# An encoder layer on one core: the weights of the last product prepared at another place, and in part not prepared

## The chip, the core and the metric

The kernel runs on one core of a Trainium2 chip. The metric is the device time of one execution in microseconds (us). The kernel before took 1651.42 us (median of 3 runs, 1650.65 to 1651.42). The engines of the core are named as in the profile: PE multiplies matrices (PEld is its loading of weights), DVE, ACT and POOL compute element by element, SP only issues transfers (DMA).

## The reference

Two sequences of 512 tokens with 1024 channels go through one layer, each with a memory of 256 tokens:

```python
xn = rmsnorm(x); h = xn @ w_in                     # u, q, k, v, xq and three gates g
branches = (s5(u), diff_attention(q, k, v), cross_attention(xq, mem))
merged = sum(sigmoid(g[n]) * (branches[n] @ w_up[n]) for n in range(3))
x = x + merged @ w_out
gate, up = split(rmsnorm(x) @ w_ffn_in)            # 2 x 2816 columns
y = rmsnorm(x + (silu(gate) * up) @ w_ffn_out)
```

All numbers are 32-bit floats. "The last product" below is `(silu(gate) * up) @ w_ffn_out`, 2816 x 1024 weights on 1024 tokens.

## The kernel before

Everything is held with channels along the 128 partitions and tokens along the free dimension; a matrix is a row of tiles of 128 x 1024 (512 columns for each sequence). A product of two 32-bit matrices is made of three matmuls: each operand is split into a high part, rounded by ACT (`split`, L128, or L131 where it is scaled), and a low part, what is left, subtracted by DVE (L129, or L132 where it is scaled); the matmuls high x high, high x low and low x high are summed in PSUM (L61).

The stages follow each other in the order of the code: projections, the S5 branch, cross attention, differential attention, the gated merges (`merge_units`: 24 tiles, the last eight ending in `mg`, L726, and its split `mgh`, `mgl`), the product with `w_out`, the FFN (22 steps of `for i in range(KFF)`), the last product, and a tail with four leftover tiles and the last norm.

The FFN and the last product use a form of the product of 2 x 2 blocks that takes seven block products in place of eight. One step of the FFN makes four blocks of 128 x 512 (gate and up, both sequences) out of seven sums of products; the step's activations go to DRAM (`aD[i]`, "aD<-ac"). For the last product two such tiles, 2p and 2p+1, form a pair of operands (p = 0 to 8): `act_pair` loads them back ("fa" and "fb"), `quad_sums` forms four sums of their quarters ("ts": L907, L909, L910 on DVE, L908 on POOL), and `quad_split` splits the seven blocks into "th" and "tl".

The weights of the last product come in 36 pieces (m, p): the 2 x 2 blocks A11, A12 (output tile m) and A21, A22 (output tile m+4), 128 x 128 each, against pair p. A piece gives 21 matmuls (seven products of three). `VISITS` puts the pieces into 12 visits of 2, 3 or 4 pieces; a visit keeps its seven sums in seven PSUM banks, and at its end ACT copies one of them ("p", L1041), DVE adds the others (`summed`, L1035: "u", "gf", "p", "up", "nsq"), and POOL adds the four results to the output tiles ("y", L1143). While a visit's matmuls run, DVE drains the visit before it; and since only pairs 0 and 1 are ready when the last product begins, the early visits have a pair of operands made beside them too (`pair_in`), one after visit 1, two after visit 3, one each after visits 4, 6 and 7.

A piece needs seven weight blocks: A11, A12, A22 and the four sums S1 to S4. The kernel before prepares all seven of every piece long before, in `prepare`: a piece is loaded ("raw", 4 x 128 columns), its A11, A12, A22 are split (L131, L132, "hl", 128 x 384) and stored to DRAM ("wD<-hl", 384 KB), POOL forms the four sums in place (L424 to L427, 128 x 128 each), and these are split (128 x 512) and stored (512 KB). `half_piece` takes half of that, one split with its store, wherever it is called: 16 pieces beside cross attention, 11 beside the gated merges, 9 beside the FFN's steps 1 to 18 (`NPREP`). In the last product a piece is then only two loads ("w<-wD", 384 and 512 KB) straight into the weight buffers.

The order of instructions on an engine is the order of the code, except where the scheduler of the framework moves work forward: it fills an engine's queue by what it expects to be ready, under the constraint of the buffers, while PE keeps its written order in the attentions and the merges that go with them, and from the last FFN step through the last product (`PE.on`). Buffers come from pools, and a pool on the right side takes room that another pool gave back: the "ts" buffers of the last two-and-a-half FFN steps are opened only after the pool "pq" of `prepare` is closed, at step 19. SP issues every transfer in its own queue.

## Time and profile before

One execution was profiled. Its own time was 1648.71 us, 2.71 us less than the median of the runs; its span, from the first to the last record, 1646.9 us, leaves 1.8 us around it.

| | us of the span | share |
|---|---|---|
| PE busy | 1597.5 | 97% |
| PE not busy | 49.4 | 3% |
| DVE busy | 1175.2 | 71% |
| ACT busy | 633.5 | 38% |
| POOL busy | 550.4 | 33% |
| mean granted clock of PE | 0.988 | |

PE is the engine to look at first. Where it is busy for the whole of a stage, nothing on the other engines costs anything; where it is not, or where its granted clock falls below 1, time is lost. The stages, by their place in the span: cross attention 412 to 522 us, differential attention 522 to 740 (its end to 787), the last merges 787 to 876, `w_out` to 996, the FFN to 1417, the last product to 1588, the tail to 1647.

### The profile page before, as it was taken

The page shows a single profiled execution, that of the slowest core. Times are in us where ns is not written, and L with a number is a line of the kernel's source. Part 1 is how long each engine was busy: PE and PEld are TensorE (multiplying, and loading weights), DVE is VectorE, ACT ScalarE, POOL GpSimd, SP SyncE. Part 2 cuts the span into 40 slices and gives each one's busy share as a digit, 9 for nine tenths or more (in the row PEclk, how much of TensorE's full clock was granted, in tenths as well). Part 3 has the DMA queues.
Part 4 walks back from the last instruction along what each step waited for, and adds up shares of the span by engine and source line. Part 5 has one row for each costly group of instructions (what it writes and reads, how often), then busy time and mean ns, then how long its engine had stood idle before and what let it go on. Part 6 is the DMA issues. An engine that isn't in the chain of part 4 may idle for free.

```text
span 1646.9 us, 21707 instructions
## 1 busy us (share of the span) xinstructions
PE 1597.5 (97%) x7812; PEld 1317.8 (80%) x7812; DVE 1175.2 (71%) x1860; ACT 633.5 (38%) x1130; POOL 550.4 (33%) x444
## 2 busy tenths in 40 slices
PE   7999999899999999999989999999999999999997
PEld 5788788788897778777767886888888887888887
DVE  7957897154775676766576657898998888886545
ACT  6534323245554355564233433333233332331122
POOL 0001100000333221200555344666666665344242
PEclk9999999999999999999999998999999999999998
DMA  9354343737664110145785542433333322887632
GB/s 366 123 165 150 110 157 111 233 120 249 234 231 150 52 59 22 54 144 178 241 301 166 163 130 64 145 131 105 129 118 106 119 99 94 291 322 243 213 116 102
DMA packets 109355, 259.61 MB, mean 158 GB/s; under 512 B 14016, under 2 KB 42432, under 8 KB 109248
## 3 DMA queue, kind: packets, MB, share of 16 engines
q1 hardware_dynamic: 109248, 258.23, 46.1%
q8 instruction: 61, 1.00, 0.3%
q14 instruction: 46, 0.38, 0.1%
HBM read 174.85 MB, written 83.33 MB: 157 GB/s over the span
## 4 chain that ended last, share of the span: by engine, by line
PE 79%; DVE 10%; DMA 3%; issue 2%; POOL 2%; ACT 2%; SPq 1%; DVEq 0%; POOLq 0%; ACTq 0%
PE bkmm L61 68%; PE bktr L61 3%; PE bksc L61 2%; PE bkoo L61 2%; PE bktr L64 2%; DVE wl L129 2%; DVE st L1492 1%; PE bktr L1474 1%; POOL mg L726 1%; POOL up L1089 1%; DMA yt<-bD 1%; DVE hl L132 1%; DVE xt L243 0%; DMA wD<-hl 0%; DMA raw<-in_w_fo 0%
## 5 line engine op out<-in xcount | busy, mean ns | idle before, releaser
L61 PE MATMUL bkmm<-xh,wh 128*128 128x512 f32 x640 | 255.4, 399 | 1.2 <-ACT wh L128 1.2
L61 PE MATMUL bkmm<-xh,wl 128*128 128x512 f32 x640 | 250.9, 393 | 2.3 <-DVE wl L129 2.3
L61 PE MATMUL bkmm<-xl,wh 128*128 128x512 f32 x640 | 250.6, 392 | 0.0
L61 PE MATMUL bkmm<-tl,wh 128*128 128x512 f32 (+1 forms) x621 | 243.3, 392 | 3.3 <-DVE tl L129 3.3
L61 PE MATMUL bkmm<-th,wl 128*128 128x512 f32 (+1 forms) x621 | 241.5, 390 | 3.4 <-DVE wl L129 3.4
L61 PE MATMUL bkmm<-th,wh 128*128 128x512 f32 (+1 forms) x621 | 243.2, 392 | 0.0
L129 DVE TENSOR_TENSOR wl<-wf,wh 128x1024 fp32r<-128x1024 f32 (+1 forms) x133 | 152.0, 1143 | 71.8 <-ACT wh L128 63.4
L128 ACT CAST wh<-wf 128x1024 fp32r<-128x1024 f32 (+1 forms) x133 | 117.7, 885 | 204.2 <-PE bkmm L61 138.0
L424 POOL TENSOR_TENSOR raw<-raw 128x128 f32<-128x128 f32 x36 | 22.3, 620 | 400.3 <-DVE hl L132 396.9
L61 PEld LDWEIGHTS bkmm<-xh,wh 128*128 128x128 f32 x640 | 120.3, 188 | 32.0 <-issue 7.9
L61 PEld LDWEIGHTS bkmm<-xh,wl 128*128 128x128 f32 x640 | 120.2, 188 | 29.6 <-DVE wl L129 3.1
L61 PEld LDWEIGHTS bkmm<-tl,wh 128*128 128x128 f32 x621 | 117.7, 190 | 28.4 <-DVE tl L129 4.4
L61 PEld LDWEIGHTS bkmm<-th,wl 128*128 128x128 f32 x621 | 117.2, 189 | 27.7 <-DVE wl L129 3.9
L61 PE MATMUL bkmm<-th,w 128*128 128x512 f32 x432 | 139.2, 390 | 0.0
L61 PEld LDWEIGHTS bkmm<-xl,wh 128*128 128x128 f32 x640 | 120.4, 188 | 22.4 <-issue 0.4
L61 PEld LDWEIGHTS bkmm<-th,wh 128*128 128x128 f32 x621 | 117.6, 189 | 25.6 <-ACT wh L128 1.2
L1089 POOL TENSOR_TENSOR up<-up,acc 128x512 f32<-128x512 f32 x44 | 84.6, 1942 | 93.6 <-DVE up L1035 93.6
L61 PEld LDWEIGHTS bkmm<-th,w 128*128 128x128 f32 x432 | 81.1, 188 | 17.5 <-DVE up L1035 0.7
L132 DVE SCALAR_TENSOR_TENSOR hl<-raw,hl 128x384 fp32r<-128x384 f32 (+1 forms) x72 | 72.9, 1016 | 24.0 <-ACT hl L131 23.9
L487 ACT ACTIVATE e<-bksc,nb 128x512 f32<-128x512 f32 (+1 forms) x96 | 58.8, 615 | 70.0 <-DVE nb L482 51.7
L61 PE MATMUL bkmm<-tl,w 128*128 128x512 f32 x216 | 84.1, 389 | 0.0
L61 PE MATMUL bkmm<-yh,wh 128*128 128x512 f32 x192 | 78.0, 407 | 3.3 <-DVE gl L722 2.9
(628 smaller groups left out, 3524.7 us busy)
## 6 DMA issues: line engine op xcount, KB each, us to landing
wf<-in_w_in SPq DMA_DIRECT2D x40, 512.0 KB, 3.9
wD<-hl SPq DMA_DIRECT2D x36, 512.0 KB, 2.9
w<-wD SPq DMA_DIRECT2D x36, 512.0 KB, 4.5
wD<-hl SPq DMA_DIRECT2D x36, 384.0 KB, 2.9
w<-wD SPq DMA_DIRECT2D x36, 384.0 KB, 3.4
gD<-gt SPq DMA_DIRECT2D x24, 512.0 KB, 2.9
gl<-gD SPq DMA_DIRECT2D x24, 512.0 KB, 4.0
wf<-in_w_fg SPq DMA_DIRECT2D x22, 512.0 KB, 3.5
```

The source lines that it names most:

```text
L61: return self.put(self.eng.matmul(*args, **kw))
L64: return self.put(self.eng.transpose(*args, **kw))
L128: h = S.copy(hi, src)
L129: l_ = V.tensor_tensor(out=lo, in0=src, in1=hi.bitcast(F32), op=ALU.subtract)
L132: l_ = V.scalar_tensor_tensor(out=lo, in0=src, scalar=scale, in1=hi.bitcast(F32), op0=ALU.mult, op1=ALU.subtract)
L424: PO.tensor_tensor(out=a22, in0=a21, in1=a22, op=ALU.add)
L487: last_x = S.activation(out=e, in_=sc, func=AF.Exp, bias=nb, scale=scale, accum_out=sm)
L726: PO.tensor_tensor(out=mg[m], in0=mg[m], in1=gt, op=ALU.add)
L1089: PO.tensor_tensor(out=up, in0=up, in1=accs[s], op=ALU.mult)
L1474: PE.matmul(ps[:, g * P : (g + 1) * P], w_[:, gg * P : (gg + 1) * P], u_[:, 8 * o + gg, :], start=True, stop=True)
L1492: V.tensor_tensor(out=sv[:, :, :, i], in0=p_, in1=q_, op=ALU.add)
```

## The change

`PREPARED` says how many blocks of a piece are prepared in each visit: seven for the two pieces of visit 0, four (the sums S1 to S4 alone) for the 32 pieces of visits 1 to 10, none for the two pieces of visit 11. All of this is done beside cross attention, in 36 half pieces (one more call at its beginning); `raw` gets four buffers and is loaded three pieces ahead. Beside the merges and the FFN nothing is prepared any more, and the pool "pq" is closed before differential attention.

In the last product `weights7` takes the place of `prepared`. For a piece with four blocks it loads the raw A11, A12, A22 into one of the two buffers of "acc" (128 KB + 64 KB), loads the sums from `wD` (512 KB), and one piece later, ahead of its matmuls, splits the raw blocks on ACT (L131) and DVE (L132) into the weight buffers. For the last two pieces POOL forms the sums there as well. Loads are issued two pieces ahead. Pair 4 is made after the first piece of visit 3, not after its end.

The diff, with the unchanged ends of functions left out:

```diff
@@ -36,7 +36,7 @@
           (2, 6, 9), (3, 7, 9))
 NPAIR = 9
 
-NPREP = (16, 27)
+PREPARED = (7, 4, 4, 4, 4, 4, 4, 4, 4, 4, 4, 0)
 
 NG = (7, 5, 7)
 ROUND = 12582912.0
@@ -393,39 +393,56 @@
 
 
 
-    pieces = [(m, p) for m, lo_, hi_ in VISITS for p in range(lo_, hi_)]
-    wD = {mp: drp.tile([P, 7, 2, P], F32, name=f"wD{mp[0]}_{mp[1]}") for mp in pieces}
-
-    def prepare(es_, pieces_):
+    pieces = [(m, p, PREPARED[v]) for v, (m, lo_, hi_) in enumerate(VISITS) for p in range(lo_, hi_)]
+    wD = {(m, p): drp.tile([P, n, 2, P], F32, name=f"wD{m}_{p}") for m, p, n in pieces if n}
+
+    def raw_in(raw, m, p, whole=True):
+
+        f = slice(2 * p * P, (2 * p + 2) * P)
+        nc.sync.dma_start(raw[:, 1:3], a["w_fo"][m, :, f].rearrange("p (a n) -> p a n", n=P))
+        if whole:
+            return nc.sync.dma_start(raw[:, 0::3], a["w_fo"][m + 4, :, f].rearrange("p (a n) -> p a n", n=P))
+        f = slice((2 * p + 1) * P, (2 * p + 2) * P)
+        return nc.sync.dma_start(raw[:, 3], a["w_fo"][m + 4, :, f])
+
+    def raw_sums(raw):
+
+        a21, a11, a12, a22 = (raw[:, i] for i in range(4))
+        PO.tensor_tensor(out=a22, in0=a21, in1=a22, op=ALU.add)
+        PO.tensor_tensor(out=a21, in0=a11, in1=a21, op=ALU.subtract)
+        PO.tensor_tensor(out=a11, in0=a22, in1=a11, op=ALU.subtract)
+        PO.tensor_tensor(out=a12, in0=a12, in1=a11, op=ALU.subtract)
+
+    def prepare(es_):
         pq = es_.enter_context(tc.tile_pool(name="pq", bufs=1, side="right", reuse_waits="tile"))
-        raws = []
-
-        def load(m, p):
-            raw = pq.tile([P, 4, P], F32, tag="raw", name="raw", bufs=2)
-            f = slice(2 * p * P, (2 * p + 2) * P)
-            with queued():
-                nc.sync.dma_start(raw[:, 1:3], a["w_fo"][m, :, f].rearrange("p (a n) -> p a n", n=P))
-                nc.sync.dma_start(raw[:, 0::3], a["w_fo"][m + 4, :, f].rearrange("p (a n) -> p a n", n=P))
-            raws.append(raw)
-
-        load(*pieces_[0])
+        todo_, raws = [x_ for x_ in pieces if x_[2]], []
+
+        def load():
+            if len(raws) < len(todo_):
+                raws.append(pq.tile([P, 4, P], F32, tag="raw", name="raw", bufs=4))
+                with queued():
+                    raw_in(raws[-1], *todo_[len(raws) - 1][:2])
+
+        def part(n_, j, w_):
+            m, p, _ = todo_[n_]
+            k = w_.shape[1]
+            hl = pq.tile([P, k, 2, P], F32R, tag=f"hl{k}", name="hl", bufs=k // 2)
+            split(hl[:, :, 0], hl[:, :, 1], w_, scale=0.5)
+            nc.sync.dma_start(wD[m, p][:, j : j + k], hl.bitcast(F32))
+
+        for _ in range(3):
+            load()
         yield
-        for n_, (m, p) in enumerate(pieces_):
-            raw = raws[n_]
-            if n_ + 1 < len(pieces_):
-                load(*pieces_[n_ + 1])
-            for j, w_ in ((4, raw[:, 1:4]), (0, raw)):
-                n = w_.shape[1]
-                hl = pq.tile([P, n, 2, P], F32R, tag=f"hl{n}", name="hl")
-                split(hl[:, :, 0], hl[:, :, 1], w_, scale=0.5)
-                nc.sync.dma_start(wD[m, p][:, j : j + n], hl.bitcast(F32))
-                if j:
-                    a21, a11, a12, a22 = (raw[:, i] for i in range(4))
-                    PO.tensor_tensor(out=a22, in0=a21, in1=a22, op=ALU.add)
-                    PO.tensor_tensor(out=a21, in0=a11, in1=a21, op=ALU.subtract)
-                    PO.tensor_tensor(out=a11, in0=a22, in1=a11, op=ALU.subtract)
-                    PO.tensor_tensor(out=a12, in0=a12, in1=a11, op=ALU.subtract)
+        for n_, (m, p, k) in enumerate(todo_):
+            load()
+            if k == 7:
+                part(n_, 4, raws[n_][:, 1:4])
+                raw_sums(raws[n_])
                 yield
+            part(n_, 0, raws[n_])
+            if n_ + 1 < len(todo_) and todo_[n_ + 1][2] == 4:
+                raw_sums(raws[n_ + 1])
+            yield
 
     def half_piece(behind_=()):
         with ExitStack() as es_:
@@ -534,7 +551,7 @@
     xcol = phase.enter_context(tc.tile_pool(name="xcol", bufs=2, reuse_waits="tile"))
 
     pes = ExitStack()
-    prep = prepare(pes, pieces[: NPREP[0]])
+    prep = prepare(pes)
     next(prep)
 
 
@@ -659,6 +676,8 @@
             S.copy(osb, oo)
             nc.sync.dma_start(bD[2, h, :, s * L : (s + 1) * L], osb)
         half_piece(last_e)
+        if i == -AHEAD:
+            half_piece(last_e)
     while queue:
         fill(6)
     assert next(prep, None) is None
@@ -850,11 +869,8 @@
         if i > 2 and steps[i - 3][2] == 3:
             normed(i - 3)
     aes.close()
-    prep = prepare(pes, pieces[NPREP[0] : NPREP[1]])
-    next(prep)
     while queue:
         fill(24)
-        half_piece()
     assert next(todo, None) is None
     PE.on = False
     phase.close()
@@ -869,11 +885,6 @@
     for m in range(KD):
         for _ in merge_units(1, b1, m, last=True):
             pass
-        half_piece()
-        if m < 6:
-            half_piece()
-    assert next(prep, None) is None
-    pes.close()
 
 
 
@@ -1062,12 +1073,7 @@
             w = next(wg)
             next(wg)
             next(wg)
-        if i == 1:
-            prep = prepare(pes, pieces[NPREP[1] :])
-            next(prep)
-        elif i == KFF - 3:
-            assert next(prep, None) is None
-            pes.close()
+        if i == KFF - 3:
             open_tags(ses, side="right", ts=1)
             open_tags(fes, ts2=1)
         if i == KFF - 1:
@@ -1090,8 +1096,6 @@
             V.scalar_tensor_tensor(out=ac[:, cs], in0=ac[:, cs], scalar=1.0, in1=gf, op0=ALU.add, op1=ALU.mult)
             V.tensor_tensor(out=ac[:, cs], in0=ac[:, cs], in1=up, op=ALU.mult)
         nc.sync.dma_start(aD[i], ac)
-        if 1 <= i < KFF - 3:
-            half_piece((last_t, last_sum))
 
 
 
@@ -1108,25 +1112,54 @@
 
     n_w = 0
 
-    def prepared(m, p):
-
-        nonlocal n_w, last_w
+    def w_room(n):
+        nonlocal n_w
+        n_w += 1
+        tag = ("wf", "wf", "wh", "wl", "wh", "wl")[n_w % 6]
+        return wp.tile([P, DM], F32R, tag=tag, name="w7")[:, : n * 2 * P].rearrange("p (j h c) -> p j h c", h=2, c=P)
+
+    def weights7(m, p, n):
+
+        nonlocal last_w
+        wa, ws_ = w_room(3), w_room(4)
+        raw = None
+        if n < 7:
+            raw = new_acc().rearrange("p (a n) -> p a n", n=P)
+            last_w = raw_in(raw, m, p, n == 0)
+        if n:
+            last_w = nc.sync.dma_start(ws_.bitcast(F32), wD[m, p][:, 0:4])
+        if n == 7:
+            last_w = nc.sync.dma_start(wa.bitcast(F32), wD[m, p][:, 4:7])
+        yield
+        if n < 7:
+            split(wa[:, :, 0], wa[:, :, 1], raw[:, 1:4], scale=0.5)
+        if n == 0:
+            raw_sums(raw)
+            yield
+            split(ws_[:, :, 0], ws_[:, :, 1], raw, scale=0.5)
         res = {}
-        for j, names in ((4, ("A11", "A12", "A22")), (0, ("S3", "S2", "S4", "S1"))):
-            tag = ("wf", "wf", "wh", "wl", "wh", "wl")[n_w % 6]
-            n_w += 1
-            n = len(names)
-            w_ = wp.tile([P, DM], F32R, tag=tag, name="w7")[:, : n * 2 * P]
-            last_w = nc.sync.dma_start(w_.bitcast(F32), wD[m, p][:, j : j + n].rearrange("p j h c -> p (j h c)"))
+        for w_, names in ((wa, ("A11", "A12", "A22")), (ws_, ("S3", "S2", "S4", "S1"))):
             for i, nm in enumerate(names):
-                res[nm] = w_[:, 2 * i * P : (2 * i + 1) * P], w_[:, (2 * i + 1) * P : (2 * i + 2) * P]
-        return res
-
+                res[nm] = w_[:, i, 0], w_[:, i, 1]
+        made.append(res)
+
+
+    made, coming = [], [weights7(*x_) for x_ in pieces]
+    next(coming[0])
+    next(coming[1])
+    next(coming[0], None)
+    n_p = 0
     for v, (m, lo_, hi_) in enumerate(VISITS):
         ps = [bank() for _ in range(6)] + [aux()]
         for p in range(lo_, hi_):
+            if n_p + 2 < len(pieces):
+                next(coming[n_p + 2])
+            for g in coming[n_p + 1 : n_p + 2]:
+                for _ in g:
+                    pass
             th, tl = pairs[p]
-            w = prepared(m, p)
+            w = made[n_p]
+            n_p += 1
             if v < 4 and p == 1:
                 with queued():
                     for t in (m, m + 4):
@@ -1136,6 +1169,8 @@
                 PE.matmul(p_, wh, th[:, o], start=(p == lo_), stop=False)
                 PE.matmul(p_, wh, tl[:, o], start=False, stop=False)
                 PE.matmul(p_, wl, th[:, o], start=False, stop=(p == hi_ - 1))
+            if v == 3 and p == 0:
+                pair_in()
         ps = iter(ps)
         c11, c12, c21, c22 = quadrants(ps, next(ps), ("nsq", "nsq"))
         for c_, t, s in ((c11, 0, 0), (c22, 4, 1), (c21, 4, 0), (c12, 0, 1)):
@@ -1147,7 +1182,7 @@
         elif v == 1:
             with tc.issue_after(last_sum.ins):
                 pair_in()
-        for _ in range({3: 2, 4: 1, 6: 1, 7: 1}.get(v, 0)):
+        for _ in range({3: 1, 4: 1, 6: 1, 7: 1}.get(v, 0)):
             pair_in()
         if v == 8:
```

Three places show how the built programs differ. The first is DVE's queue in the last merges, where `gl<-gl,bkmm` (L722) takes a merge's result out of PSUM, `wl` is the low half of the next merge's weights and `hl` that of a prepared piece. Before:

```order
L129 TENSOR_TENSOR wl<-wf,wh 128x512
L722 SCALAR_TENSOR_TENSOR gl<-gl,bkmm 128x512
L132 SCALAR_TENSOR_TENSOR hl<-raw,hl 128x4x128
L132 SCALAR_TENSOR_TENSOR hl<-raw,hl 128x3x128
L722 SCALAR_TENSOR_TENSOR gl<-gl,bkmm 128x512
L129 TENSOR_TENSOR wl<-wf,wh 128x512
```

and now, where the line of the merge is L741:

```order
L129 TENSOR_TENSOR wl<-wf,wh 128x512
L741 SCALAR_TENSOR_TENSOR gl<-gl,bkmm 128x512 x2
L129 TENSOR_TENSOR wl<-wf,wh 128x512
L741 SCALAR_TENSOR_TENSOR gl<-gl,bkmm 128x512 x2
L129 TENSOR_TENSOR wl<-wf,wh 128x512
```

The splits of the pieces are gone, and with them what POOL and SP did for them. The second place is DVE's queue in the FFN. Before, the sums of pairs 0 and 1 ("ts") stood in the third last step, between the additions of PSUM banks (`u`, `gf`) and the next split of weights:

```order
L1035 TENSOR_TENSOR u_12383<-bkmm,p_12368 128x512
L907 TENSOR_TENSOR ts<-fa 128x512 x2
L909 TENSOR_TENSOR ts<-fb,ts 128x512
L1035 TENSOR_TENSOR gf<-bkmm,p_12368 128x512
L909 TENSOR_TENSOR ts<-fb,ts 128x512
L910 TENSOR_TENSOR ts<-fb,ts 128x512
L129 TENSOR_TENSOR wl<-wf,wh 128x1024
```

Now their buffers are free from the start of the FFN, and the same sums (L918 to L921) stand in its first steps, as soon as the tiles of activations that they read exist; here those of pair 0 between the end of step 1 (`ac<-ac,up`, which is stored as tile 1 and read back as `fb`) and the second half of step 2:

```order
L1097 TENSOR_TENSOR ac<-ac,up 128x512
L1046 TENSOR_TENSOR u_9744<-bkmm,p_9729 128x512
L1046 TENSOR_TENSOR gf<-bkmm,p_9729 128x512
L1093 TENSOR_TENSOR gf<-gf,acc 128x512
L129 TENSOR_TENSOR wl<-wf,wh 128x1024
L1096 SCALAR_TENSOR_TENSOR ac<-ac,gf 128x512
L1046 TENSOR_TENSOR u_9774<-bkmm,u_9744 128x512
L920 TENSOR_TENSOR ts<-fb,ts 128x512
L921 TENSOR_TENSOR ts<-fb,ts 128x512
L1046 TENSOR_TENSOR p_9789<-bkmm,u_9744 128x512
L1046 TENSOR_TENSOR up<-bkmm,u_9774 128x512
L129 TENSOR_TENSOR wl<-ws,wh 128x1024
```

The sums of pair 1 stand in the same way in steps 3 and 4: four operations after the end of step 2 and four after that of step 3. What moved is the place at which DVE waits for tiles of activations that have gone to DRAM and come back. The third place is DVE's queue at the end of visit 0 of the last product. Before, it held the visit's additions and then the split of pair 2:

```order
L1035 TENSOR_TENSOR p_12888<-bkmm,u_12882 128x512
L1035 TENSOR_TENSOR up<-bkmm,u_12886 128x512
L1035 TENSOR_TENSOR nsq<-bkmm,u_12886 128x512
L1035 TENSOR_TENSOR nsq<-bktr,p_12888 128x512
L129 TENSOR_TENSOR tl<-fa,th 128x512
L129 TENSOR_TENSOR tl<-fb,th 128x1024
L129 TENSOR_TENSOR tl<-ts,th 128x1024 x2
```

and now:

```order
L1046 TENSOR_TENSOR p_12734<-bkmm,u_12728 128x512
L132 SCALAR_TENSOR_TENSOR w_12668<-acc,w_12668 128x3x128
L1046 TENSOR_TENSOR up<-bkmm,u_12732 128x512
L1046 TENSOR_TENSOR nsq<-bkmm,u_12732 128x512
L132 SCALAR_TENSOR_TENSOR w_12695<-acc,w_12695 128x3x128
L1046 TENSOR_TENSOR nsq<-bktr,p_12734 128x512
L129 TENSOR_TENSOR tl<-fa,th 128x512
L129 TENSOR_TENSOR tl<-fb,th 128x1024
L129 TENSOR_TENSOR tl<-ts,th 128x1024 x2
L132 SCALAR_TENSOR_TENSOR w_12763<-acc,w_12763 128x3x128
L132 SCALAR_TENSOR_TENSOR w_12792<-acc,w_12792 128x3x128
```

The splits of raw weights (L132, out of "acc") stand among the additions and behind the split of the pair, one for each of the coming pieces.

## The prediction

> **What bounds the kernel now.** I read the shares of the page first, then the span by stages, then the waits of the stages in which PE is not full. The first two lines are the span and PE's share:
>
> ```profile
> span 1646.9 us, 21707 instructions
> PE 1597.5 (97%) x7812; PEld 1317.8 (80%) x7812; DVE 1175.2 (71%) x1860; ACT 633.5 (38%) x1130; POOL 550.4 (33%) x444
> ```
>
> PE is idle for 49.4 us in all, so a change that leaves the matmuls alone can win no more than this and what a low clock costs. The stages show where that lies (columns: length, busy time of the engines with the count of their operations, granted clock, DMA share, GB/s):
>
> ```profile
> core 0: us, PE busy (x) PEld busy (x) DVE busy (x) ACT busy (x) POOL busy (x), PEclk, DMA share, GB/s
> 412.00:522.00 110.00, 107.01 (x635) 93.38 (x634) 78.59 (x218) 61.35 (x156) 31.87 (x65) 1.00 0.64 224
> 787.00:876.00 89.00, 81.53 (x340) 63.51 (x339) 59.17 (x71) 29.23 (x53) 54.92 (x53) 0.97 0.83 278
> 876.00:996.00 120.00, 116.19 (x510) 94.62 (x508) 73.13 (x79) 48.49 (x61) 47.57 (x30) 0.97 0.45 142
> 996.00:1348.00 352.00, 351.84 (x1541) 290.53 (x1542) 307.09 (x330) 109.22 (x147) 230.35 (x148) 0.99 0.34 115
> 1348.00:1417.00 69.00, 65.55 (x282) 53.87 (x281) 58.90 (x68) 26.43 (x34) 30.91 (x17) 0.98 0.34 111
> 1417.00:1488.50 71.50, 71.50 (x315) 58.81 (x314) 64.89 (x76) 16.84 (x22) 35.79 (x24) 1.00 0.92 336
> ...
> 1517.00:1531.30 14.30, 14.30 (x65) 11.84 (x64) 9.88 (x12) 5.12 (x6) 5.09 (x4) 1.00 0.82 268
> ```
>
> The FFN to 1348 us and the last product's first five visits (1417 to 1488.5) are full: nothing can be won there, only lost. FFN matmuls come at 352.00 / 1541 = 0.2284 us each. At that pitch the 340 of the last merges take 77.7 us of their 89.0, so 11.3 are lost; the 282 of the FFN's end 64.4 of 69.0, 4.6 lost; the 510 of `w_out` 116.5 of 120.0, 3.5 lost, 3% of the stage. The change takes its preparation out of the first two of these and puts work into cross attention and the last product; the last product's early visits have DVE busy for 64.89 of 71.5 us, so that is where I looked for the price.
>
> **The merges lose 22 half pieces.** What the engines waited for there (us in total, times, longest), and then the chain of the stage:
>
> ```profile
> POOL raw L424 <- DVE hl L132: 113.8, 11, 92.2
> ACT hl L131 <- DMA wD<-hl: 21.3, 5, 6.0
> ACT hl L131 <- POOL raw L427: 20.3, 6, 5.1
> DVE hl L132 <- ACT hl L131: 19.0, 11, 3.2
> PE bkmm L61 <- DVE wl L129: 3.3, 3, 2.3
> PE bkmm L61 <- DVE gl L722: 2.9, 2, 2.5
> ...
> by line: issue 23.5%; POOL mg L726 14.4%; DMA raw<-in_w_fo 8.6%; DVE hl L132 8.5%; DMA wD<-hl 5.8%; DMA wf<-in_w_up 5.8%; POOL raw L426 5.7%; DMA yt<-bD 4.6%; POOL raw L425 4.1%; DVE wl L129 3.9%; POOL raw L424 3.6%; POOL raw L427 2.2%; ACT
> ```
>
> ACT waits for the stores and POOL's sums of a piece, DVE behind it for ACT's half, and PE at last for `wl` and `gl`, which stand in DVE's queue behind the pieces' splits. The chain runs over the pieces' transfers, splits and sums. All of these go: 22 splits on ACT and on DVE, 44 POOL additions, the loads and the stores. Late next is what `w_out`, without any piece, loses too: 3% of 77.7, 2.3 us. So I take -(11.3 - 2.3) = **-9.0 us**; the ends are -11.3 (nothing left) and -3.0 (the tiles `yt` from DRAM and POOL's `mg` hold the stage as before, and half of PE's own named waits of 6.2 us goes).
>
> **The seam between FFN and last product.** One wait makes it:
>
> ```profile
> PE bkmm L61 <- DVE wl L129: 3.4, 1, 3.4
> ```
>
> It stands near the end of the FFN, where PE waits for weights whose split comes late in DVE's queue behind the sums of pairs 0 and 1, which the buffers forced into the third last step. Those sums now stand in the first steps. The wait goes, and with it the 1.2 us of slow matmuls behind it: **-4.6 us** (ends -3.4 and -4.6).
>
> **The FFN loses 18 half pieces and gets the sums early.** These rows of the FFN price it (count, busy us, mean ns; then transfers, KB and us to landing):
>
> ```profile
> L1090 DVE SCALAR_TENSOR_TENSOR ac<-ac,gf 128x512 f32<-128x512 f32 x37 | 47.2, 1277 | 10.6 <-ACT ac L1088 10.6
> L1087 DVE TENSOR_TENSOR gf<-gf,acc 128x512 f32<-128x512 f32 x36 | 27.8, 771 | 1.1
> L129 DVE TENSOR_TENSOR wl<-wf,wh 128x1024 fp32r<-128x1024 f32 x18 | 24.8, 1376 | 0.0
> L1035 DVE TENSOR_TENSOR gf<-bkmm,p 128x512 f32<-128x512 f32 x36 | 24.4, 679 | 0.0
> L132 DVE SCALAR_TENSOR_TENSOR hl<-raw,hl 128x384 fp32r<-128x384 f32 x9 | 14.8, 1642 | 0.0
> L132 DVE SCALAR_TENSOR_TENSOR hl<-raw,hl 128x512 fp32r<-128x512 f32 x8 | 14.2, 1774 | 0.0
> ...
> aD<-ac SPq DMA_DIRECT2D x18, 512.0 KB, 2.7
> ...
> fa<-aD SPq DMA_DIRECT2D x2, 512.0 KB, 3.6
> fb<-aD SPq DMA_DIRECT2D x2, 512.0 KB, 3.3
> ```
>
> The splits that go (14.8 + 14.2 = 29.0 us of DVE, and ACT's and POOL's share) win nothing, since PE is full beside them. The sums cost: a tile is stored and loaded back, 2.7 + 3.3 us for `fb` and 2.7 + 3.6 for `fa`, and in DVE's new order few operations stand between a step's end and the sum that needs its tile. After step 1 there are six (0.68 + 0.68 + 0.77 + 1.38 + 1.28 + 0.68 = 5.5 us), so DVE waits 0.5 us; after step 2 four (3.5 us), wait 2.8; after step 3 four, wait 2.5. Queued behind each are an addition that frees a PSUM bank and the next `wl`, for which PE waits. In sum 5.8 us; DVE would be busy for (307.09 - 29.0) / 352 = 0.79 of the stage, so a fifth of a wait falls into time in which it had nothing to do: **+4.6 us**. The ends: 0 if DVE has that slack at just these places (21% of a 16 us step is 3.4 us), and 11.6 if the round trip through DRAM takes half again as long.
>
> **Cross attention gets 36 half pieces for 32.** Its rows:
>
> ```profile
> L132 DVE SCALAR_TENSOR_TENSOR hl<-raw,hl 128x512 fp32r<-128x512 f32 x16 | 11.0, 687 | 1.7 <-ACT hl L131 1.5
> L132 DVE SCALAR_TENSOR_TENSOR hl<-raw,hl 128x384 fp32r<-128x384 f32 x16 | 8.8, 552 | 2.3 <-ACT hl L131 2.3
> ...
> L131 ACT ACTIVATE hl<-raw 128x512 fp32r<-128x512 f32 x16 | 10.1, 632 | 4.4 <-POOL raw L427 4.4
> L131 ACT ACTIVATE hl<-raw 128x384 fp32r<-128x384 f32 x16 | 8.3, 519 | 2.5 <-DMA wD<-hl 2.5
> ...
> L424 POOL TENSOR_TENSOR raw<-raw 128x128 f32<-128x128 f32 x16 | 7.4, 460 | 286.5 <-DVE hl L132 283.1 <-DVE nb L484 3.4
> ```
>
> In place of 16 + 16 splits there are 34 wide and 2 narrow ones: DVE 34 x 0.687 + 2 x 0.552 - 19.8 = +4.7 us, ACT +4.1, POOL 72 additions more at 0.46 = +33 us, and 34 loads of 256 KB with 34 stores of 512 and 2 of 384 move 8.5 MB more than 16 of each did (224 GB/s x 110 us = 24.6 MB in all). The stage of 110 us has room for it (DVE 83, ACT 65, POOL 65, DMA about 0.85); what stays on the path are the last pieces, whose splits now stand before the first weights of differential attention. I take two of them, 2 x (0.63 + 0.69) = **+2.6 us**; ends 0 and 8.8 (all of DVE's and ACT's addition in a row).
>
> **The last product gets the splits.** Each of 34 pieces costs ACT 0.52 us, where it is idle for three quarters, and DVE one L132 of 128x384. POOL's 8 extra sums, for the last two pieces, come where the last visits leave it room. The loads come down from 896 to 704 KB a piece and are issued one piece earlier than needed before; no PE wait on them is in the trace, and I cost them at nothing. For DVE the price of a split depends on POOL: 0.55 us in cross attention, 1.64 in the FFN, where POOL is busy for 230 of 352 us. Operations of the same kind in the stage itself:
>
> ```profile
> L129 DVE TENSOR_TENSOR tl<-fa,th x5: 714/1754/1790, 1428.0 to 1478.5; 128x512 fp32r<-128x512 f32 x5
> ...
> L1143 POOL TENSOR_TENSOR y<-y,nsq 128x512 f32<-128x512 f32 x22 | 30.7, 1416 | 0.0
> ```
>
> the first take 0.71 or about 1.75 us, which I read as alone or beside an addition of POOL's, the second row. POOL is busy for 35.79 of the 71.5 us, half, so a split costs 0.55 + 0.5 x 1.09 = 1.10. Fourteen pieces are split in visits 0 to 4: 15.4 us, against 71.5 - 64.89 = 6.6 us in which DVE is idle. The rest, 8.8 us, makes PE wait, since the additions that free its banks and the pairs' splits stand behind: **+8.8 us**. From visit 5 on DVE is busy for at most 69% (9.88 of 14.30 us in visit 7, the last row of the stages), and I add nothing. The ends are 0 (0.55 each, 7.7 us, an excess of 1.1 that one piece's lead, 21 matmuls or 4.8 us, covers) and +16.4 (1.64 each).
>
> [...]
>
> **The sum**, against the profiled execution: -9.0 - 4.6 + 4.6 + 2.6 + 8.8 = +2.4 us. That execution took 1648.71 us, the median of the runs is 2.71 higher: 1651.42 + 2.4 = 1653.8, said as 1654. This is near what a measurement can tell from no change (0.2%, 3.3 us), so the likeliest case lies on both sides of that bound.
>
> **Rivals.** (1) DVE covers the splits of the last product: POOL's additions start only when DVE has made their operand, so the two may fall out of step, and each split costs 0.55. With its term at 0 the sum is -6.4, 1645 us; if the early sums of the FFN are hidden too, -11.0, 1640. For it: in the profile no PE wait exists in the stage at 91% of DVE; against it: the splits stand at fixed places of the queue, so idle time elsewhere does not serve them. It decides from a mean split of 0.7 us down. [...] (3) The merges don't come free: the chain keeps `mg`, `yt` and the weights, term -3.0, sum +8.4, 1660. Against it is that the pieces' own rows make up most of the named chain. (4) Cross attention overflows, at its upper end: +8.6, 1660.
>
> **How the numbers follow.** The sum's own case, 1649 to 1658 us, gets 0.50, of which 0.22 lies within 0.2% and 0.28 above; rival 1 0.26; rival 2 0.12; rivals 3 and 4 together 0.12, a little of it within 0.2% where two errors cancel. Faster 0.28, same 0.22, slower 0.50. The range leaves out the far end of rival 1 and both ends together: 1643 to 1663.
>
> **What would show it.** In the trace after: 787 to 876 us shorter by some 9 us, with no POOL `raw`; no PE wait at the FFN's end; DVE waits on `fb<-aD` of 2 to 3 us in FFN steps 2 to 4 with a PE wait on `wl` behind them; in the last product PE waits on DVE in visits 0 to 4, L132 at 1.1 us in the mean, the stage 9 us longer. If the last product stays at its length, or if the merges stay at theirs, the sign is wrong.

## The result

The changed kernel took 1652.86 us (median of 20 runs), the kernel before 1650.76 us in the runs beside them (20): the ratio is 1.0012, with a 95% interval of 1.0004 to 1.0021. It is slower by 2.1 us: less than the 0.2% that the prediction gave as about what can be told from no change, but the interval, from twenty runs of each, leaves no change out. Ratios and medians are of undisturbed runs; one run of v_hybrid below, which took 2524.55 us at a granted clock of 0.637, is not among them.

The page of the changed kernel begins like this:

```profile
span 1652.8 us, 21658 instructions
PE 1599.8 (97%) x7812; PEld 1316.8 (80%) x7812; DVE 1162.2 (70%) x1860; ACT 637.6 (39%) x1130; POOL 542.7 (33%) x444
```

DVE and POOL do a little less than before, since the half pieces in the FFN had been the dear ones (a split of DVE took 1.64 to 1.77 us in the mean there, 0.55 to 0.69 in cross attention), and PE is idle for 53.0 us in place of 49.4. The sum says little; the stages say where it went. A stage is read here from the first matmul of one kind to the first of the next. For the changed kernel these rows of the matmul line give the places (count, shortest, median and longest ns, then first and last start in us): scores of cross attention, scores of differential attention, merges, `w_out`, last product.

```profile
L61 PE MATMUL bksc<-mkvh,qh x32: 277/281/366, 412.4 to 515.5; 128*128 128x256 f32 x32
L61 PE MATMUL bksc<-rh x64: 492/493/501, 553.2 to 771.7; 64*128 64x512 f32 x64
L61 PE MATMUL bkmm<-yh,wh x192: 387/389/500, 737.6 to 887.3; 128*128 128x512 f32 x192
L61 PE MATMUL bkmm<-mgh,wh x128: 389/389/389, 888.0 to 974.4; 128*128 128x512 f32 x128
L61 PE MATMUL bkmm<-th,w x432: 387/389/628, 1411.8 to 1592.6; 128*128 128x512 f32 x144
```

The same rows of every profile, subtracted, make this table (us; "cross" reaches to the first score of differential attention, the FFN from its first matmul to that of the last product, "last" to the start of its last matmul). The second profile of the changed kernel and the experiments are told below.

| kernel | start | cross | diff. | merges | w_out | FFN | last | tail |
|---|---|---|---|---|---|---|---|---|
| before | 411.7 | 133.2 | 184.5 | 163.0 | 87.0 | 436.0 | 171.6 | 59.9 |
| changed | 412.4 | 140.8 | 184.4 | 150.4 | 87.1 | 436.7 | 181.5 | 59.5 |
| changed, again | 411.5 | 139.2 | 184.4 | 150.3 | 87.0 | 436.4 | 179.9 | 59.3 |
| only transfers beside merges | 411.9 | 136.1 | 184.5 | 154.6 | 87.1 | 435.9 | 171.7 | 59.2 |
| no sums beside merges | 414.4 | 135.8 | 184.5 | 159.7 | 88.2 | 436.1 | 171.6 | 59.6 |
| fewer half pieces | 413.0 | 133.3 | 184.4 | 150.3 | 87.0 | 435.7 | 186.5 | 59.5 |
| pair sums at step 19 | 414.3 | 140.4 | 184.4 | 150.5 | 87.0 | 433.3 | 182.0 | 59.5 |
| pair sums at step 10 | 412.8 | 138.5 | 184.4 | 149.9 | 87.0 | 432.2 | 180.6 | 59.1 |
| low halves by ACT | 412.4 | 139.9 | 184.4 | 149.8 | 87.0 | 435.6 | 173.7 | 59.5 |

Three stages change. The merges are 12.6 us shorter, cross attention with its end is longer, and the last product is 8 to 10 us longer; the FFN is as long as it was. In the two profiles side by side the change is 5.9 us, in the medians 2.1. The profiled execution of the changed kernel was 1.7 us above its median, and that of before was one with a short cross attention: the two kernels that differ from it only beside the merges run the same instructions there in the same order, and took 135.8 and 136.1 us, not 133.2.

The stages of the changed kernel (the columns are those of the prediction's table of stages). The first row is of the kernel before: its merges from 787 us to their end. The row from 795.20 us is the same part of the changed kernel, which comes there 8.2 us later:

```profile
787.00:892.40 105.40, 97.93 (x408) 76.93 (x407) 71.52 (x84) 33.87 (x58) 65.05 (x59) 0.97 0.79 265
...
412.00:522.00 110.00, 107.44 (x637) 93.57 (x635) 82.01 (x218) 62.58 (x157) 72.47 (x125) 1.00 0.84 281
522.00:530.00 8.00, 3.40 (x11) 2.14 (x10) 5.04 (x9) 2.87 (x5) 4.86 (x5) 0.82 0.81 292
530.00:545.00 15.00, 15.00 (x59) 12.12 (x59) 5.82 (x10) 2.83 (x4) 6.51 (x6) 0.87 0.03 11
795.20:888.00 92.80, 92.40 (x408) 75.58 (x407) 48.88 (x62) 22.91 (x36) 40.10 (x15) 1.00 0.48 156
1348.00:1412.00 64.00, 63.38 (x280) 52.16 (x279) 49.64 (x58) 25.53 (x32) 26.33 (x15) 1.00 0.31 105
1412.00:1488.00 76.00, 70.65 (x296) 55.68 (x295) 73.20 (x86) 25.27 (x37) 34.97 (x22) 0.98 0.78 268
```

The same 408 matmuls of the merges take PE 92.8 us in place of 105.4, at full clock and with 0.4 us of idle time, and the DMA share fell from 0.79 to 0.48. The end of the FFN is full. The two bad places are the eight us after 522, in which PE is busy for 3.40, and the first visits of the last product, in which DVE is busy for 73.20 of 76 us.

What PE waited for, first around the end of cross attention, then in the FFN with the seam, then in the last product:

```profile
PE bkmm L61 <- DVE t L706: 2.8, 1, 2.8
PE bkoo L61 <- ACT xpTh L128: 1.0, 1, 1.0
PE bkoo L61 <- DVE xpTl L129: 0.8, 1, 0.8
...
PE bkmm L61 <- DVE wl L129: 3.5, 6, 1.6
PE bkmm L61 <- DVE tl L129: 3.5, 2, 1.9
...
PE bkmm L61 <- DVE w L132: 2.2, 2, 1.1
PE bkmm L61 <- DVE up L1046: 1.8, 1, 1.8
PE bkmm L61 <- ACT w L131: 0.6, 1, 0.6
```

The wait of 3.4 us at the seam has become six short waits on `wl` in the FFN, five of them in its first steps (`tl` belongs to the start of the FFN and was there before, 3.3 us); in the last product PE waits for the split blocks themselves and for a bank that DVE drains late.

### The profile page after: what moved, and what is told of

Read it like the earlier page. It is cut to its first block, busy times and chain, and to the rows that moved or that the text cites. A ratio compares the mean times of both kernels' runs of the same rounds, so it can differ in the third digit from the quotient of the medians.

```text
span 1652.8 us, 21658 instructions
## 1 busy us (share of the span) xinstructions
PE 1599.8 (97%) x7812; PEld 1316.8 (80%) x7812; DVE 1162.2 (70%) x1860; ACT 637.6 (39%) x1130; POOL 542.7 (33%) x444
## 4 chain that ended last, share of the span: by engine, by line
PE 69%; DVE 14%; DMA 6%; issue 5%; POOL 3%; ACT 2%; SPq 1%; DVEq 0%; ACTq 0%; POOLq 0%
PE bkmm L61 60%; PE bktr L61 2%; DVE tl L129 2%; PE bksc L61 2%; DVE wl L129 2%; PE bkoo L61 1%; DMA raw<-in_w_fo 1%; PE bktr L64 1%; POOL up L1095 1%; DVE st L1527 1%; PE bktr L1509 1%; POOL mg L745 1%; DMA yt<-bD 1%; DMA fb<-aD 1%; DMA aD<-ac 1%
## 5 line engine op out<-in xcount | busy, mean ns | idle before, releaser
L129 DVE TENSOR_TENSOR wl<-wf,wh 128x1024 fp32r<-128x1024 f32 (+1 forms) x133 | 141.7, 1065 | 70.2 <-ACT wh L128 59.9
L61 PE MATMUL bkmm<-th,w 128*128 128x512 f32 x432 | 142.2, 394 | 5.4 <-DVE w L132 2.2
L745 POOL TENSOR_TENSOR mg<-mg,gl 128x1024 f32<-128x1024 f32 x16 | 43.9, 2744 | 139.2 <-DVE gl L741 139.2
L128 ACT CAST wh<-ws 128x1024 fp32r<-128x1024 f32 x44 | 46.1, 1051 | 102.8 <-PE bkmm L61 72.9
```

The source lines that it names most:

```text
L61: return self.put(self.eng.matmul(*args, **kw))
L128: h = S.copy(hi, src)
L129: l_ = V.tensor_tensor(out=lo, in0=src, in1=hi.bitcast(F32), op=ALU.subtract)
L745: PO.tensor_tensor(out=mg[m], in0=mg[m], in1=gt, op=ALU.add)
```

## The experiments

**The changed kernel again.** No edit.

> The changed kernel once more, for a second profile of it. In the first pair of profiles the stages differ like this, by the first matmul of each: cross attention with its end 133.2 -> 140.8 us (+7.6), differential attention -0.1 + 0.6, the merges 163.0 -> 150.4 (-12.6), w_out 87.0 -> 87.1, the FFN 436.0 -> 436.7 (+0.7), the last product 171.8 -> 181.6 (+9.8). If these are properties of the program, each stage repeats within 1 us, and the ratio to before is 1.001 to 1.003; if they are of the one execution, stages move by several us between the two profiles of the same program.

The ratio was 1.0015 (1.0002 to 1.0028). Start, differential attention, merges, `w_out` and FFN repeat within 1 us; cross attention and the last product came 1.6 us shorter each. So these two, in which PE stalls, also vary from one execution to the next, a little more than I had expected, but the signs of the three changes and most of their sizes are of the program.

**What the merges had lost.** Two kernels on the kernel before, for the 11 pieces beside the merges alone. The first leaves POOL's 44 sums out:

```diff
-                if j:
+                if j and not no_sums:
                     a21, a11, a12, a22 = (raw[:, i] for i in range(4))
...
-    prep = prepare(pes, pieces[NPREP[0] : NPREP[1]])
+    prep = prepare(pes, pieces[NPREP[0] : NPREP[1]], True)
```

> The kernel before, with the 44 additions of POOL left out for the 11 pieces that are prepared beside the merges (the sums of these pieces are then not formed and the outputs are not the reference's); their loads, splits and stores stay. The merges took 163.0 us with all of it and 150.4 without any. If the chain runs through POOL (ACT's second split waits for the sums, and the sums for mg), most of the 12.6 us go: 150 to 155 us. If the splits before `wl` and `gl` in DVE's queue and the stores are the cause, the stage stays at 158 or more.

The second leaves the splits out as well and stores the raw blocks twice:

```diff
-                hl = pq.tile([P, n, 2, P], F32R, tag=f"hl{n}", name="hl")
-                split(hl[:, :, 0], hl[:, :, 1], w_, scale=0.5)
-                nc.sync.dma_start(wD[m, p][:, j : j + n], hl.bitcast(F32))
-                if j:
+                if no_split:
+                    for h_ in range(2):
+                        nc.sync.dma_start(wD[m, p].rearrange("p j h c -> p (j h c)")[:, (2 * j + n * h_) * P : (2 * j + n * h_ + n) * P], w_.rearrange("p a c -> p (a c)"))
+                else:
+                    hl = pq.tile([P, n, 2, P], F32R, tag=f"hl{n}", name="hl")
+                    split(hl[:, :, 0], hl[:, :, 1], w_, scale=0.5)
+                    nc.sync.dma_start(wD[m, p][:, j : j + n], hl.bitcast(F32))
+                if j and not no_split:
...
```

> The kernel before, with only the transfers of the preparation left beside the merges: the 11 pieces are loaded and stored twice as they are (the same bytes), without the 22 splits on ACT and DVE and without POOL's sums, so that the outputs are not the reference's. Without POOL's sums alone the merges took 159.7 us, without any of it 150.4. If the transfers hold the merges' own loads back, 156 to 160 us; if it was the splits in DVE's and ACT's queues, 150 to 152.5.

The merges took 159.7 and 154.6 us, against 163.0 with everything and 150.3 with nothing. POOL's sums are not most of the loss: 159.7 is on the side that I had given to the splits and stores. Between these two neither of my readings holds alone, 154.6 lying above the 150 to 152.5 of the splits and below the 156 to 160 of the transfers. Taken away in this order, and by one profile each, POOL's sums are worth 3.3 us, the 22 splits on ACT and DVE 5.1, the transfers 4.3. Part of the first two is the clock: over the 408 matmuls it was granted at 0.97 before, 0.98 without the sums, and 1.00 from there on. The whole kernels stood at 0.9982 (0.9972 to 0.9992) and 0.9959 (0.9942 to 0.9977) of the kernel before.

**Cross attention with less.**

```diff
-PREPARED = (7, 4, 4, 4, 4, 4, 4, 4, 4, 4, 4, 0)
+PREPARED = (7, 4, 4, 4, 4, 4, 4, 4, 0, 0, 0, 0)
```

> The changed kernel with PREPARED = 7, then 4 for visits 1 to 7, 0 for visits 8 to 11: 26 half pieces beside cross attention in place of 36, and 12 pieces whose sums POOL makes in the last product. If the tail of the preparation is what holds the start of differential attention, its first score comes at 545 to 547 us in place of 553.2, 6 to 8 us won; the late visits have room on DVE and POOL and cost 0 to 4. If the order of DVE's queue at the end of cross attention is the cause, whatever is prepared, the first score stays at 550 or later.

The first score of differential attention came at 546.3 us, the stage took 133.3. Where the preparation ends is seen in the rows of DVE's split, first of the changed kernel, with the chain behind PE's wait (start and length in us), then of this one, with PE's stretch behind it:

```profile
L132 DVE SCALAR_TENSOR_TENSOR hl<-raw,hl x36: 548/692/984, 416.1 to 526.6; 128x512 fp32r<-128x512 f32 x34, 128x384 fp32r<-128x384 f32 x2
...
513.05 3.57 DMA raw<-in_w_fo
...
516.75 0.95 POOL raw L411
...
521.93 0.92 POOL raw L411
...
525.44 0.47 POOL raw L414
525.93 0.64 ACT hl L131
526.60 0.70 DVE hl L132
...
527.95 0.72 DVE t L706
528.71 16.38 PE bkmm L61 x60
```

```profile
L132 DVE SCALAR_TENSOR_TENSOR hl<-raw,hl x26: 550/690/985, 416.6 to 494.0; 128x512 fp32r<-128x512 f32 x24, 128x384 fp32r<-128x384 f32 x2
...
520.00:530.00 10.00, 8.23 (x37) 6.37 (x36) 3.77 (x7) 2.44 (x4) 1.88 (x2) 1.00 0.25 80
```

The last split of the changed kernel begins at 526.6 us, after the stage has ended, and the operations `t` that lead to the first scores stand behind it in DVE's queue. It is late because a load, POOL's sums of the last three pieces (from 516.75 to 525.9 us, almost without a gap) and ACT's half stand ahead of it. With fewer half pieces the last split begins at 494.0, and PE keeps its clock. So the number of half pieces sets the stall, not the order of DVE's queue at the end. The other half of the expectation failed: the last product took 186.5 us, 5 to 6.6 more than in the changed kernel, where I had said 0 to 4. Ten more pieces with POOL's sums and wide splits are not free even in the late visits. The ratio to before, 1.0016 (1.0006 to 1.0025), is that of the changed kernel.

**The FFN with the pair sums held back**, to the third last step and to step 10 (N is 19 and 10):

```diff
+        if i == N:
+            late = last_t, last_sum
         if i == KFF - 1:
-            acts = [act_pair(0), act_pair(1, "ts2")]
+            with tc.issue_after(late[0].ins), tc.issue_after(late[1].ins):
+                acts = [act_pair(0), act_pair(1, "ts2")]
```

> The changed kernel with the sums of pairs 0 and 1 held back to the third last step of the FFN, where they stood before; nothing is prepared beside the FFN. If the early sums cost what the trace says, PE's waits in the first FFN steps go (-5.3 us). The wait at the seam (4.6 us before) comes back in full if the sums alone made it, so that the FFN stays at 436 us; it comes back by less than 1.5 us if the split of the last prepared piece, which stood in the same queue, made it, and the FFN takes 431 to 433 us.

> The changed kernel with the sums of pairs 0 and 1 held back to FFN step 10: late enough that the tiles have long come back from DRAM, early enough that nothing is due. If the waits for the tiles (early) and the crowd in DVE's queue (late) are what the FFN loses, both go: 431 to 432 us in place of 436.4 (changed) and 433.3 (held back to step 19), the whole 0.3% faster than the changed kernel. If the sums cost DVE time wherever they stand, the FFN stays above 434.

(For N = 19 the line stands in an `if` that is there already.) The FFN took 433.3 and 432.2 us, against 435.6 to 436.7 in the four profiles with the early sums and nothing prepared beside the FFN, and 436.0 before. The whole stood at 0.9998 (0.9986 to 1.0010) with step 19, and at 0.9981 (0.9967 to 0.9995) with step 10: this one edit makes the changed kernel faster than the kernel before. In the changed kernel's first FFN steps DVE waits for the tiles that come back from DRAM, and PE for weights behind it; with the sums at step 10 one short wait on `wl` is left between cross attention and the end:

```profile
DVE ts L920 <- DMA fb<-aD: 3.7, 2, 2.1
DVE ts L918 <- DMA fa<-aD: 2.4, 2, 2.0
...
PE bkmm L61 <- DVE wl L129: 2.9, 5, 1.6
```

```profile
PE bkmm L61 <- DVE wl L129: 0.6, 1, 0.6
```

At step 19 the sums alone cost 1.1 us: the one wait on `wl` at the seam is 1.7 us there, against 0.6 in all with the sums at step 10. The kernel before lost 3.8 against the best, so its seam was made by the sums together with the prepared pieces; sums without preparation make a third of it. These are differences of single profiles, and the four with the early sums differ by 1.1 us among themselves.

**The last product without the splits on DVE.** ACT makes both halves, the low one as a second copy:

```diff
-            split(wa[:, :, 0], wa[:, :, 1], raw[:, 1:4], scale=0.5)
+            for j in range(2):
+                S.activation(out=wa[:, :, j], in_=raw[:, 1:4], func=AF.Copy, scale=0.5)
```

> The changed kernel, but in the last product ACT makes both halves of a raw block (the low half is a second copy of the scaled block, so the subtraction is left out and the outputs are not the reference's); the 34 splits on DVE (L132) are gone. If DVE's time in the early visits is what made the last product longer, it goes from 181.6 to 172 to 174 us and the whole is 7 to 10 us faster than the changed kernel. If the raw loads with their short rows, the two buffers or the place of ACT's copies are the cause, the last product stays at 179 us or more.

The stage took 173.7 us and the whole 1644.08, 8.1 less than the changed kernel beside it. Here are the 14 splits of the changed kernel in the first visits (by form: busy us and mean ns; by tile: shortest, median, longest). Behind them, by start and length in us, stand one split that began while POOL was busy with two additions in a row and one that began just before an addition:

```profile
L132 DVE SCALAR_TENSOR_TENSOR w<-acc,w 128x384 fp32r<-128x384 f32 x14 | 12.2, 880 | 1.5 <-ACT w L131 1.5
...
L132 DVE SCALAR_TENSOR_TENSOR w<-acc,w x14: 542/558/1637, 1422.8 to 1482.5; 128x384 fp32r<-128x384 f32 x14
...
1482.52 1.31 DVE L132 SCALAR_TENSOR_TENSOR w<-acc,w 128x384 fp32r<-128x384 f32 x1 [1.48 <-ACT w L131]
1480.45 2.96 POOL L1178 TENSOR_TENSOR y<-y,nsq 128x512 f32<-128x512 f32 x2
...
1465.79 0.55 DVE L132 SCALAR_TENSOR_TENSOR w<-acc,w 128x384 fp32r<-128x384 f32 x1
1465.94 1.54 POOL L919 TENSOR_TENSOR ts<-fb,fa 128x512 f32<-128x512 f32 x1 [4.03 <-DVE tl L129]
```

All 14 follow this pattern. The six that began while an addition of POOL was running took 1.03 to 1.64 us; the other eight, of which six met no addition and two began just before one, took 0.54 to 0.56.

The next three rows are visits 0 to 4 of the last product, of the kernel before, the changed kernel and this one; below them stand all PE waits of this kernel in the last product:

```profile
1415.40:1487.10 71.70, 71.70 (x316) 58.96 (x316) 65.09 (x77) 18.20 (x23) 34.81 (x24) 1.00 0.92 337
...
1411.80:1492.50 80.70, 75.35 (x317) 59.59 (x316) 77.90 (x92) 26.32 (x39) 36.72 (x24) 0.98 0.79 271
...
1409.10:1482.80 73.70, 72.70 (x316) 58.70 (x315) 65.84 (x78) 31.68 (x54) 36.27 (x24) 1.00 0.84 297
...
PE bkmm L61 <- DMA w<-wD: 0.6, 1, 0.6
PE bkmm L61 <- ACT w L1136: 0.4, 1, 0.4
```

The same matmuls take 73.7 us in place of 80.7: without the splits 7.0 of the 9.0 us by which visits 0 to 4 had grown are gone. DVE's time was the cause of most of it. The 2.0 us that are left are 1.0 of named waits and 1.0 by which PE is busy longer for the same matmuls; the cause of the latter stays open.

**A version from the parts.** The table of stages, read as a ledger of what each place charges, says where work costs least: nothing beside the merges, no splits in the first five visits, at most 32 or so half pieces beside cross attention, the rest beside the FFN. The first version prepares all seven blocks for visits 0 to 4, the sums for visits 5 to 10, and takes 16 pieces (31 half pieces) to cross attention and 18 to FFN steps 1 to 18:

```diff
-PREPARED = (7, 4, 4, 4, 4, 4, 4, 4, 4, 4, 4, 0)
+PREPARED = (7, 7, 7, 7, 7, 4, 4, 4, 4, 4, 4, 0)
+NCROSS = 16
...
-    prep = prepare(pes)
+    prep = prepare(pes, todo_p[:NCROSS], 3, 2)
...
+        if i == 1:
+            prep = prepare(pes, todo_p[NCROSS:], 1, 1)
...
+        if 1 <= i < KFF - 3:
+            half_piece((last_t, last_sum))
```

> All seven blocks are prepared for visits 0 to 4 (15 pieces), the four sums alone for visits 5 to 10 (19 pieces), nothing for visit 11; 31 half pieces beside cross attention, nothing beside the merges, 18 half pieces beside FFN steps 1 to 18. If the ledger of stages holds, cross attention is back at 133 to 134 us, the merges at 150.4, the FFN at 435 to 437 (PE is full beside the splits, and one pair's sums stand early, one late), the last product at 172 to 174.5 (19 splits where DVE has room): 8 to 12 us faster than before, ratio 0.993 to 0.995. If the raw split costs in the late visits what it costs in the early ones, the last product takes 177 or more and the gain is half of that.

> As v_hybrid, with the one pair's sums that stand early held back to FFN step 10. If only the waits for tiles coming back from DRAM go, the FFN is 1.5 to 3 us shorter than in v_hybrid; if DVE's queue has the slack at steps 1 and 2, it is the same within 0.5 us.

> As v_hybrid_b, but the 18 half pieces of the FFN are done in its steps 1 to 12 (two in every second step), so that their pool is given back at step 13, and the sums of both pairs stand at step 14. In v_hybrid_b the FFN took 439.4 us with one pair's sums in the third last step; the changed kernel with all sums at step 10 and no preparation took 432.2. If the crowd at the end of the FFN made the difference, 432 to 434 and the whole at a ratio of 0.991 to 0.993 to before; if DVE can't carry one and a half splits a step beside POOL, 436 or more.

> As v_hybrid_c, with 35 half pieces beside cross attention and 14 in FFN steps 1 to 14, one a step, sums of both pairs at step 16. Cross attention: 36 half pieces, 34 of them wide, cost it 6 us, 31 cost nothing; with 15 narrow and 20 wide ones between 132.5 and 137. The FFN at 432 to 433. Ratio 0.991 to 0.995.

> As v_hybrid_b, with nothing prepared for visit 10 either: 31 half pieces beside cross attention, 15 in FFN steps 1 to 15, sums of both pairs at step 16. From the stages measured: cross attention 132.5 (v_hybrid_b), merges 150.2, FFN 435 (v_hybrid_d, 14 half pieces and sums at step 16), last product 175.5 plus 1 to 3 for three more raw pieces. Together 1 to 3 us faster than v_hybrid_b, ratio to before 0.994 to 0.996. If the raw pieces of visit 10 cost more than the FFN wins, the ratio is 0.997 or more.

| version | cross | merges | FFN | last | median us | ratio to before (95%) |
|---|---|---|---|---|---|---|
| v_hybrid | 132.5 | 149.7 | 443.1 | 175.4 | 1646.66 | 0.9983 (0.9973 to 0.9992) |
| v_hybrid_b, early sums at step 10 | 132.5 | 150.2 | 439.4 | 175.5 | 1644.08 | 0.9963 (0.9948 to 0.9977) |
| v_hybrid_c, 18 half pieces in 12 steps | 132.5 | 150.4 | 453.4 | 179.3 | 1657.65 | 1.0047 (1.0034 to 1.0061) |
| v_hybrid_d, 35 half pieces beside cross attention | 142.2 | 149.8 | 435.2 | 175.5 | 1645.94 | 0.9978 (0.9968 to 0.9987) |
| v_hybrid_e, visit 10 raw, sums at step 16 | 132.4 | 150.0 | 436.3 | 176.1 | 1641.77 | 0.9948 (0.9933 to 0.9963) |

Cross attention, merges and last product came out near what the ledger said (the last product 1 us over); the FFN missed it by 7 us in the first version. My reading is that one pair's sums stood early there and waited for DRAM with DVE as full as before, and that the other's stood in the crowd of step 19. Holding the early ones back won 3.7 us, more than I had said; PE's waits on `wl` between 412 and 1600 us went from 7.0 to 5.3 us. Half pieces at one and a half a step, with both pairs' sums at step 14, were a plain mistake: PE's waits on `wl` in the FFN grew to 12.7 us, from 5.3 in v_hybrid_b, and the granted clock of the first half of the stage fell from 0.98 to 0.94. Here is that half in v_hybrid_b, then in v_hybrid_c with the waits:

```profile
970.00:1190.00 220.00, 214.32 (x937) 175.43 (x936) 189.88 (x203) 71.23 (x97) 146.68 (x110) 0.98 0.36 119
...
970.00:1190.00 220.00, 206.00 (x864) 166.84 (x863) 181.21 (x194) 68.75 (x95) 144.65 (x119) 0.94 0.38 127
...
PE bkmm L62 <- DVE wl L130: 12.7, 8, 2.9
```

DVE is busy for 181 of 220 us in v_hybrid_c, 82%, and PE waits more than in v_hybrid_b, where DVE is busy for 190: an engine's share need not be near one for its queue to be late. Beside cross attention 31 half pieces, one fewer than in the kernel before, cost nothing. With 35 the stage took 142.2 us, beyond the 137 that I had given as its end and 9.7 more than with 31: 6.4 of them are PE's idle time and 3.3 busy time at a lower clock (0.95 from 505 to 522 us, 0.50 to 532, 0.93 to 545). That is more than the 36 of the changed kernel cost, but it is one profile. PE waits for `t` behind the last splits as there, and then has half its clock:

```profile
522.00:532.00 10.00, 3.14 (x8) 2.48 (x8) 2.63 (x5) 2.04 (x4) 3.96 (x5) 0.50 0.52 206
...
PE bkmm L62 <- DVE t L708: 6.9, 1, 6.9
```

The last version keeps to both limits, 31 half pieces there and 15 in the FFN, and beats both kernels: 0.5% below the kernel before, from six runs. Its ratio is the only one of the four forecast that held. Its gain is the merges, 13.0 us shorter than before; the last product is 4.5 longer.

## Why the prediction came out as it did

The forecast was 1654 us with the likeliest case on both sides of no change; 1652.86 was measured, +2.1 us for the +2.4 of the sum. The sign of every term was right; several sizes and one path were not. By its own steps:

- **Merges, -9.0:** the mechanism held, the size was too small. The term measured -12.6, beyond the end of -11.3. The step that failed was to leave 3% of the stage lost, 2.3 us, as in `w_out`, and to count only the stretch from 787 to 876 us: the merges went on to 892.4, and those of the changed kernel take 92.8 us for the same 408 matmuls, which is 0.2274 each with hardly a wait left. That the loss had three parts, sums, splits and transfers, was not in the prediction, which spoke of one chain.
- **Seam, -4.6, and early sums, +4.6:** the two were to cancel, and the FFN changed by +0.4 and +0.7. With the sums at step 10 it takes 432.2, so the seam had cost 3.8 and the early sums 3.4 to 4.5; both sizes were nearly right. The cause given for the seam was right in part only: the sums alone make 1.1 of it at that place, and the rest needs the prepared pieces, which the prediction held to win nothing. DVE's waits at the early sums, 6.1 us in all, are near the 5.8 worked out from the round trip and the operations between, though they fall otherwise: four waits of 0.4 to 2.1 us, not three of 0.5, 2.8 and 2.5.
- **Cross attention, +2.6:** right in kind (the last pieces stand before the first weights and scores), too small: against the three profiles of the program before (133.2, 135.8, 136.1, mean 135.0) the five with 36 half pieces (138.5 to 140.8, mean 139.8) are 4.7 us longer. The step that failed was to price the tail as two splits on ACT and DVE and to leave POOL's sums out of the path, since POOL had room over the stage. In the chain above the sums of the last three pieces alone take 9.2 us, ahead of the last split. PE's idle time in the stage is 4.9 to 7.2 us in the five, 6.1 in the mean, against 3.0 in each of the three; the rest, 1.6 us, is longer busy time, part of it the lower clock behind the stall (0.82 from 522 to 530 us in the changed kernel, 0.87 to 545).
- **Last product, +8.8:** it measured +8.3 and +9.9. A split cost 0.88 in place of 1.10, with a median of 0.558, so that the overrun worked out in the same way is 12.2 - 6.6 = 5.6. PE's idle time in visits 0 to 4 is 5.4, so the way of working it out was right. What it left out is that PE is busy for 75.35 us there in place of 71.70: behind a stall the clock was lower (0.89 from 1472 to 1488 us; 0.11 of 16 us is 1.8 us). The other half of the 3.6 us stays open. Two errors cancelled in this term.
- **Rivals.** That DVE covers the splits (-6.4) fell with the PE waits on `w` and `up` (2.2 and 1.8 us on DVE). That every split pays (+16.4, the 0.12 of rival 2) fell with the median of 0.558: of the 14 splits only the six that began while an addition of POOL was running took longer, 1.03 to 1.64 us, and the eight others took 0.54 to 0.56. +16.4 would need every split to begin beside an addition; what makes a split take longer there, no run shows. That the merges don't come free fell with their -12.6. That cross attention overflows at its upper end came halfway.

That the sum was right to 0.3 us is luck: the merges' term, 3.6 us short, met cross attention's, 2.1 short, and smaller ones. The range of 1643 to 1663 says better than the sum how well the terms were known.

## What to carry to other kernels

Work moved off a stage must be priced at the place where it lands, in units of its queue's slack there and with the chain that stands ahead of it: here 31 half pieces beside cross attention cost nothing and 35 cost some 10 us in the one profile taken, and 18 beside the FFN cost 14 us more at one and a half a step than at one. When a buffer is freed early, a scheduler may move what used it forward to a point where its input is still on its way; holding the work back by hand to a quiet place was worth 4 us. And a stage that seems to have one chain may lose to three things, so that taking one away wins only its part: POOL's sums were 3.3 of the 12.6 us.

## What the runs showed of the hardware

The same stall costs its own length in one execution and 2.6 to 2.9 us more in two others. These are the rows of the end of cross attention, of the kernel before and of the one with only transfers beside the merges, which has the same program there; the last row is a narrower stretch of the second:

```profile
515.00:525.00 10.00, 7.01 (x32) 5.31 (x31) 4.36 (x10) 3.54 (x6) 2.96 (x3) 1.00 0.39 140
525.00:535.00 10.00, 10.00 (x46) 8.29 (x45) 3.95 (x8) 1.69 (x2) 4.77 (x4) 1.00 0.04 16
```

```profile
515.00:525.00 10.00, 7.01 (x26) 5.23 (x25) 4.66 (x10) 2.89 (x6) 3.33 (x4) 0.82 0.42 150
525.00:535.00 10.00, 10.00 (x38) 8.04 (x38) 4.08 (x8) 1.34 (x3) 3.90 (x4) 0.84 0.07 26
...
521.40:528.20 6.80, 6.19 (x15) 4.84 (x16) 2.60 (x6) 1.12 (x2) 2.79 (x3) 0.50 0.37 118
```

PE is busy for 7.01 of 10 us in both; in the first the granted clock stays at 1.00, in the second it is 0.82 and 0.84, and PE does 64 matmuls where it did 78. The clock does not sink to 0.8, though: for 6.8 us it is at 0.50, and PE does 15 matmuls there. Why the same idle time lowered the clock in one execution and not in the other, no run shows. The stage differs by 2.9 us between the two (133.2 and 136.1), so one profile of a kernel with a 3 us stall is not enough to price a stage to a microsecond.
